# Layer-0 attention scores: the query's low part multiplied through all 128 rows instead of through pairs of 64-row matmuls

## The chip, the cores and the metric

The kernel runs on one core of a Trainium2 chip. The metric is the device time of one execution in microseconds (us), lower is better; of several runs the median is given. The engines are named as in the profile: PE is TensorE (matmuls) and PEld its loading of weights, DVE is VectorE, ACT is ScalarE, POOL is GpSimd, SP is SyncE, which issues most DMAs.

## The reference

A two-layer transformer step over 128 context tokens and 512 latent tokens, width 1024. Layer 0 mixes tokens by differential attention: each of 8 heads has two query/key maps of 64 features, two softmaxes, and the second is subtracted from the first with a factor `lam`.

```python
def block(qb):
    logits = jnp.einsum('bqhmd,bkhmd->bhmqk', qb, k, preferred_element_type=jnp.float32) * scale
    p = jax.nn.softmax(logits, -1)
    a = p[:, :, 0] - lam * p[:, :, 1]
    return jnp.einsum('bhqk,bkhe->bqhe', a, v).astype(v.dtype)
```

Latent queries (4 blocks of 128) see 640 keys: 128 cached context keys and 512 latent ones. Context queries (one block of 128) see the 128 context keys. Layer 1 is a neighbourhood attention with 16 heads of 64 features; each layer ends with an MLP of width 4096.

## The kernel before

All large products are made in three terms: each float32 operand is split into a high part (rounded to the type `fp32r`) and a low part (the rest), and high x high, high x low and low x high are added in one PSUM bank (`mm3`, lines 119 to 121).

For the scores of layer 0 the split is packed into the array's 128 rows, since a map has only 64 features. The tile `K[:, x]` of map `x` holds the key's high part in the 64 rows that belong to the map and its low part in the other 64 rows: "stacked high and low keys". The query tile `q` has four slices. `Q[:, x]` (x is 0 or 1) has the query's high part of map `x` twice, in both halves of the rows; `Q[:, 2 + x]` has the low part of map `x` twice. So one matmul over 128 rows with `Q[:, x]` gives query-high x (key-high + key-low). What is missing, query-low x key-high, comes from a matmul over the 64 rows of the map alone.

`scores0` (line 553) makes one block: 128 queries of one head against 640 keys, for both maps. It takes two PSUM tiles `S` of two banks, one per map, and fills them in two halves of 320 keys, each by a call of `qk`: two matmuls over 128 rows (line 452, map 0 and map 1) and then two over 64 rows (line 454; rows 0 to 63 for map 0, rows 64 to 127 for map 1). There are 8 heads x 4 blocks = 32 such blocks with 8 matmuls each. `ctx_scores0` (line 604) makes the context's block, one call of `qk` with 128 keys, 8 times in all. `softmax0` then reads `S`: a maximum on DVE (line 568), the exponential on ACT (line 570), and small steps on DVE (lines 576 to 578). `trans0` transposes the result on PE (line 589) and splits it on ACT and DVE (lines 126 and 127); `pv0` multiplies it with V.

Layer 0 is not done stage by stage. The order of PE's work is written out by hand in the string `ORDER0`: score blocks (`S`, head, block), transposes (`T`), context scores (`c`), projections of q, k and v (`q`, `v`), rotations of queries and keys (`r`), pieces of the modulation (`m`, `M`) stand mixed. PE's instructions run in that order. The instructions of the other engines are put in order by the framework's scheduler. PE's score blocks run from about 82 to 393 us.

The function `qk` is also called in layer 1 (`scores1`, `ctx_scores1`), where the two low slices are one (`lo` is `(2, 2)`).

Of the kernel before, what the change touches and what calls it, by code (L numbers as in the profile page):

```python
# [18 lines left out]
P = 128  # L19
# [46 lines left out]
class Net:  # L66
# [32 lines left out]
        self.uid += 1  # L99
        return f"{s}_{self.uid}"  # L100

# [1 line left out]

    def run(self, order):
        for name in order.split():
# [6 lines left out]
    def op(self, name, fn, *needs):  # L112
        self.ops[name] = fn, needs

# [1 line left out]

    def mm3(self, out, sh, sl, mh, ml, start, stop):
        te = self.nc.tensor
# [51 lines left out]
        assert m == 48  # L170
        return order

# [1 line left out]

    def pump(self):
        if not self.queue:
# [48 lines left out]
            if kt % 2:  # L225
                self.used(4 * n + kt // 2)

# [1 line left out]

    def consts(self):  # L230
        nc, a, c = self.nc, self.a, self.cst
# [189 lines left out]
            self.done(3)  # L421
        return accs

# [1 line left out]

    def to_h(self, i, src):
        self.split(self.h[0][:, i, :], self.h[1][:, i, :], src)
# [18 lines left out]
            r = HALF[1 - x]  # L446
            nc.gpsimd.tensor_tensor(K[r, x], cr[r, x], K[r, x], ALU.subtract)

    def qk(self, out, Q, K, q, k, lo):
        te = self.nc.tensor  # L450
        for x in range(2):
            te.matmul(out[x], Q[:, x, q], k(K[:, x]), start=True, stop=False)  # L452
        for x, r in enumerate(HALF):
            te.matmul(out[x], Q[r, lo[x], q], k(K[r, x]), start=False, stop=True)  # L454

    def v_evac(self, pool, i, t, src, cache, out):
        def put(slot, s):
# [16 lines left out]
        if t == 4:  # L474
            self.out_copy(pool, src, self.o[out][:, 256 * i : 256 * i + 256], 256)

# [1 line left out]

    def qk0_evac(self, pool, i, t, src):
        nc = self.nc  # L480
# [7 lines left out]
        if t < 4:  # L488
            t2 = pool.tile([P, 256], F32, tag="t2", name=self.nm("t2"))
            five = lambda z: z.rearrange("p (m g s f) -> p m g s f", m=4, g=2, s=2)  # L490
            four = lambda z: z.rearrange("p (a b c) -> p a b c", a=2, b=2)
            s5, d5 = five(src), five(t2)
            n4 = self.sin[:, t].unsqueeze(1).to_broadcast([P, 4, 2, 16])
            c4 = self.cos[:, t].unsqueeze(1).unsqueeze(1).to_broadcast([P, 2, 2, 64])
            nc.vector.tensor_tensor(qk, four(src), c4, ALU.mult)
            nc.vector.scalar_tensor_tensor(d5[:, :, :, 0, :], s5[:, :, :, 1, :], -1.0, n4, ALU.mult, ALU.mult)
            nc.vector.tensor_tensor(d5[:, :, :, 1, :], s5[:, :, :, 0, :], n4, ALU.mult)
            nc.vector.tensor_tensor(qk, qk, four(t2), ALU.add)
            cs = slice(P + P * t, 2 * P + P * t)
        else:  # L500
            nc.scalar.copy(qk, src.rearrange("p (a b c) -> p a b c", a=2, b=2))
            nc.sync.dma_start(self.o["k0"][:, P * i : P * i + P].rearrange("p (a b) -> p a b", b=64), qk[:, 1])
            cs = slice(0, P)
# [49 lines left out]
    def scores0(self, hd, b):  # L553
        K, qs = self.QKs[hd["h"]], slice(P + P * b, 2 * P + P * b)
        s2 = [self.S().rearrange("p (a b) -> p a b", b=512) for _ in range(2)]
        for hf in range(2):
            ks = slice(P + 320 * hf, P + 320 * hf + 320)
            self.qk([s2[m][:, hf, :320] for m in range(2)], self.q0, K, qs, lambda z: z[:, ks], (2, 3))
        hd["E", b] = self.softmax0(hd, b, [s[:, :, :320] for s in s2], 640)

    def softmax0(self, hd, b, s, n):
# [42 lines left out]
    def ctx_scores0(self, hd):  # L604
        K = self.QKs[hd["h"]]
        s = self.S()
        sm = [s[:, 0:P], s[:, 512 : 512 + P]]
        self.qk(sm, self.q0, K, slice(0, P), lambda z: z[:, :P], (2, 3))
        hd["E", 4] = self.softmax0(hd, 4, sm, P)

    def ctx_pv0(self, hd):
# [163 lines left out]
            self.nc.sync.dma_start(X[:, t, :], src[t])  # L775
        return X

# [1 line left out]

    def v1(self, pool, i, t, n, c):  # L780
        m = self.M()
# [60 lines left out]
    def scores1(self, pr, b):  # L842
        nc = self.nc
        Q, K = self.QKs[pr["i"]]
        s = self.S()
        sh = [s[:, 0:384], s[:, 512:896]]
        qs = slice(P * b, P * b + P)
        if b < 3:
            kv, out = lambda z: z[:, P * b : P * b + 384], sh
        else:  # L850
            kv = lambda z: z[:, 0:640].rearrange("p (a b) -> p a b", b=P)[:, 0:5:2, :]
            out = [z.rearrange("p (a b) -> p a b", b=P) for z in sh]
        self.qk(out, Q, K, qs, kv, (2, 2))
        E = pr["E", b]
        mn = self.sml.tile([P, 2], F32, name=self.nm("mn"), tag="mn1")
        Z = self.sml.tile([P, 2], F32, name=self.nm("Z"), tag="Z1")
        for x in range(2):
            nc.vector.tensor_tensor_reduce(
                E[:, x, :], sh[x], E[:, x, :], 1.0, 3.0e38, ALU.add, ALU.min, mn[:, x : x + 1]
            )  # L860
            nc.scalar.activation(E[:, x, :], E[:, x, :], AF.Exp, bias=mn[:, x : x + 1], scale=-1.0, accum_out=Z[:, x : x + 1])
        nc.vector.reciprocal(Z, Z)
        for x in range(2):
            nc.vector.tensor_scalar(E[:, x, :], E[:, x, :], Z[:, x : x + 1], None, ALU.mult)
# [45 lines left out]
    def ctx_scores1(self, pr):  # L910
        nc, pool = self.nc, pr["pool"]
        Q, K = self.QKs[pr["i"]]
        s = self.S()
        sh = [s[:, 0:P], s[:, 512 : 512 + P]]
        qs, ks = slice(NL, NT), slice(640, 768)
        self.qk(sh, Q, K, qs, lambda z: z[:, ks], (2, 2))
        sv = s.rearrange("p (a b) -> p a b", b=512)[:, :, :P]
        mn = self.sml.tile([P, 2], F32, name=self.nm("mn"), tag="mn1")
        Z = self.sml.tile([P, 2], F32, name=self.nm("Z"), tag="Z1")
        E = pr["Ec"] = pool.tile([P, 2, P], F32, tag="Ec", name=self.nm("Ec"), bufs=1)  # L920
        nc.vector.tensor_reduce(mn, sv, AX.X, ALU.min)
        for x in range(2):
            nc.scalar.activation(E[:, x, :], sh[x], AF.Exp, bias=mn[:, x : x + 1], scale=-1.0, accum_out=Z[:, x : x + 1])
        nc.vector.reciprocal(Z, Z)
        nc.vector.tensor_tensor(E, E, Z.unsqueeze(2).to_broadcast([P, 2, P]), ALU.mult)
# [96 lines left out]
            self.pool_lo = 1  # L1022
            return late["X"], first4

# [1 line left out]

    def stats(self, st, X, t, n):
        self.nc.vector.bn_stats(st[:, t, n, :], X[:, t, 512 * n : 512 * n + 512])
# [385 lines left out]
```

## Time and profile before

| | |
|---|---|
| median of 3 runs | 1731.97 us (1730.14 to 1737.19) |
| span of the profiled execution | 1732.1 us |
| PE busy | 1645.9 us (95% of the span) |
| DVE busy | 1131.4 us (65%) |
| ACT busy | 662.1 us (38%) |
| chain that ended last | PE 75%, DVE 14%, issue 4%, POOL 4%, ACT 3% |

The profile is of one execution and gives no time of it other than the span, which lies 0.1 us over the median of the runs; so the span is taken as its time. The start of a matmul in the trace is the moment it begins; its end is modelled, and matmuls overlap in the pipeline, so what a matmul costs is read from the distance between the starts of two that follow each other and not from its duration. A timeline merges instructions of the same line that follow each other into one row with their count. A bracket at a row's end is the engine's idle time before it, with what ended it.

### The profile page before, as it was taken

To read this page: it belongs to the slowest core of one execution; us is meant where nothing else is said; L and a number is where in the kernel's file an instruction comes from. 1 tells how busy PE (TensorE), PEld (TensorE's weight loads), DVE (VectorE), ACT (ScalarE), POOL (GpSimd) and SP (SyncE) were. 2 spreads that over 40 slices of the span, in tenths; PEclk is the share of its full clock that TensorE was granted. 3 is DMA by queue.
4 is the path that set the end of the run, shared out by engine and by line. 5 is a ranking of instruction groups with operands and counts; after the bars stand their busy time and mean duration, and the time that the engine had idled before them with its cause. 6 is when DMAs were issued, how large, how long until landed. Compare 5 with 4: busy or idle time off the path is not lost.

```text
span 1732.1 us, 25928 instructions
## 1 busy us (share of the span) xinstructions
PE 1645.9 (95%) x10026; PEld 1455.4 (84%) x10026; DVE 1131.4 (65%) x2015; ACT 662.1 (38%) x1338; POOL 594.5 (34%) x457
## 2 busy tenths in 40 slices
PE   8999999999699999999998999998889999999997
PEld 5788888777698988989887889997779898898996
DVE  4788778765848789798557577868685343242338
ACT  2456545643531322221324565655353132131321
POOL 2111012113722337154247243342383133424322
PEclk9999999989899999999999999999989999999999
DMA  8432334233144445454223222223123131212221
GB/s 328 147 118 84 100 113 148 80 112 108 57 133 151 159 146 172 142 164 144 77 83 118 89 78 79 77 85 133 61 92 106 59 98 50 97 56 91 81 66 61
DMA packets 59086, 187.96 MB, mean 109 GB/s; under 512 B 7396, under 2 KB 14034, under 8 KB 57938
## 3 DMA queue, kind: packets, MB, share of 16 engines
q1 hardware_dynamic: 55890, 174.89, 31.3%
q0 software_dynamic: 3072, 11.40, 1.8%
q8 instruction: 79, 1.29, 0.3%
q14 instruction: 45, 0.37, 0.1%
HBM read 176.25 MB, written 7.40 MB: 106 GB/s over the span
## 4 chain that ended last, share of the span: by engine, by line
PE 75%; DVE 14%; issue 4%; POOL 4%; ACT 3%; DMA 1%; SPq 0%; DVEq 0%; POOLq 0%; ACTq 0%
PE M L119 14%; PE M L121 14%; PE M L120 14%; PE S L121 8%; PE S L119 7%; PE S L120 7%; DVE wl L196 4%; PE S L452 2%; PE S L454 2%; POOL wl L196 2%; DVE hlo L127 1%; PE M L589 1%; PE M L259 1%; DVE X L1038 1%; POOL X L1078 1%
## 5 line engine op out<-in xcount | busy, mean ns | idle before, releaser
L196 POOL TENSOR_TENSOR wl<-rw,wh 128x512 fp32r<-128x512 f32 x209 | 345.3, 1672 | 591.4 <-ACT wh L194 541.0
L194 ACT CAST wh<-rw 128x1024 fp32r<-128x1024 f32 x192 | 196.9, 1050 | 348.3 <-PE M L121 268.5
L121 PE MATMUL S<-hhi,wl 128*128 128x320 f32 (+1 forms) x944 | 293.4, 311 | 6.1 <-DVE wl L196 4.7
L119 PE MATMUL S<-hhi,wh 128*128 128x320 f32 (+1 forms) x944 | 292.7, 310 | 0.0
L120 PE MATMUL S<-hlo,wh 128*128 128x320 f32 (+1 forms) x944 | 291.9, 309 | 0.0
L119 PE MATMUL M<-wh,uhi 128*128 128x512 f32 x640 | 249.6, 390 | 1.0 <-ACT uhi L126 1.0
L121 PE MATMUL M<-wh,ulo 128*128 128x512 f32 x640 | 249.3, 389 | 0.3
L120 PE MATMUL M<-wl,uhi 128*128 128x512 f32 x640 | 249.2, 389 | 0.0
L196 DVE TENSOR_TENSOR wl<-rw,wh 128x512 fp32r<-128x512 f32 x175 | 208.9, 1213 | 52.3 <-ACT wh L194 51.3
L119 PE MATMUL M<-wh,hhi 128*128 128x256 f32 (+1 forms) x640 | 202.4, 316 | 9.3 <-DVE tmp L1161 8.4
L121 PE MATMUL M<-wh,hlo 128*128 128x256 f32 (+1 forms) x640 | 196.4, 307 | 3.8 <-DVE hlo L127 3.8
L120 PE MATMUL M<-wl,hhi 128*128 128x256 f32 (+1 forms) x640 | 196.2, 307 | 1.8 <-DVE wl L196 1.8
L121 PEld LDWEIGHTS S<-hhi,wl 128*128 128x128 f32 x944 | 178.9, 189 | 10.1 <-DVE wl L196 8.3
L119 PEld LDWEIGHTS S<-hhi,wh 128*128 128x128 f32 x944 | 179.3, 190 | 0.2
L120 PEld LDWEIGHTS S<-hlo,wh 128*128 128x128 f32 x944 | 179.1, 190 | 0.2
L293 DVE SCALAR_TENSOR_TENSOR jk<-wm,cb 128x1024 bf16<-128x1024 f32 x96 | 142.5, 1484 | 1.5
L121 PEld LDWEIGHTS M<-wh,ulo 128*128 128x128 f32 x640 | 120.2, 188 | 26.3 <-DVE ulo L127 1.1
L119 PEld LDWEIGHTS M<-wh,uhi 128*128 128x128 f32 x640 | 120.2, 188 | 26.2 <-ACT uhi L126 1.9
L120 PEld LDWEIGHTS M<-wl,uhi 128*128 128x128 f32 x640 | 120.1, 188 | 24.6
L119 PEld LDWEIGHTS M<-wh,hhi 128*128 128x128 f32 x640 | 124.2, 194 | 18.6 <-DVE tmp L1161 8.9
L1225 DVE SCALAR_TENSOR_TENSOR r<-S,r 128x640 f32<-128x640 f32 (+1 forms) x62 | 48.4, 781 | 137.8 <-ACT r L1224 137.7
L121 PEld LDWEIGHTS M<-wh,hlo 128*128 128x128 f32 x640 | 123.8, 193 | 11.7 <-DVE hlo L127 7.0
(280 smaller groups left out, 3026.6 us busy)
## 6 DMA issues: line engine op xcount, KB each, us to landing
rw<-in_w SPq DMA_DIRECT2D x192, 512.0 KB, 4.2
wm<-in_wmodT SPq DMA_DIRECT2D x48, 512.0 KB, 3.6
rw<-in_wmod SPq DMA_DIRECT2D x32, 512.0 KB, 4.5
wm<-in_wmod SPq DMA_DIRECT2D x8, 1024.0 KB, 10.5
gate<-gates POOLq DMA_DIRECT2D x6, 512.0 KB, 5.0
X<-in_xT SPq DMA_DIRECT2D x8, 320.0 KB, 11.1
X<-in_xn SPq DMA_DIRECT2D x5, 512.0 KB, 5.4
x<-X SPq DMA_DIRECT2D x5, 512.0 KB, 2.8
```

The costliest lines, as they stand in the source:

```text
L119: te.matmul(out, sh, mh, start=start, stop=False)
L120: te.matmul(out, sh, ml, start=False, stop=False)
L121: te.matmul(out, sl, mh, start=False, stop=stop)
L127: nc.vector.tensor_tensor(lo, src, hi, ALU.subtract)
L194: keep(nc.scalar.copy(hi, r))
L196: keep(eng.tensor_tensor(lo[:, k], r[:, k], hi[:, k], ALU.subtract))
L259: self.nc.tensor.matmul(acc[32 * j : 32 * j + 32, :256], self.sc[:, 4 * r + j, :], w[:, j, :], start=r == 0, stop=r == 1, tile_position=(0 ...
L293: op = nc.vector.scalar_tensor_tensor(jk, ws[t], 1.0, cb[:, x, :], ALU.mult, ALU.mult, accum_out=mc[:, t, x : x + 1])
L452: te.matmul(out[x], Q[:, x, q], k(K[:, x]), start=True, stop=False)
L454: te.matmul(out[x], Q[r, lo[x], q], k(K[r, x]), start=False, stop=True)
L589: nc.tensor.transpose(t[:, P * (j - j0) : P * (j - j0) + P], E[:, P * j : P * j + P], self.idf)
L1225: nc.vector.scalar_tensor_tensor(rv, src, 0.0, rv, ALU.max, ALU.mult)
```

## The change

`qk` now makes, for each map in turn, two matmuls over all 128 rows: one with the query's high slice and one with its low slice, both against the stacked keys. The 64-row form lives on as `qk_rows`, for layer 1 alone, with the same instructions as before. In place of query-low x key-high the new form adds query-low x (key-high + key-low). The tiles, what is written into them, and the order string stay.

```diff
-    def qk(self, out, Q, K, q, k, lo):
+    def qk(self, out, Q, K, q, k):
+        te = self.nc.tensor
+        for x in range(2):
+            te.matmul(out[x], Q[:, x, q], k(K[:, x]), start=True, stop=False)
+            te.matmul(out[x], Q[:, 2 + x, q], k(K[:, x]), start=False, stop=True)
+
+    def qk_rows(self, out, Q, K, q, k):
         te = self.nc.tensor
         for x in range(2):
             te.matmul(out[x], Q[:, x, q], k(K[:, x]), start=True, stop=False)
         for x, r in enumerate(HALF):
-            te.matmul(out[x], Q[r, lo[x], q], k(K[r, x]), start=False, stop=True)
+            te.matmul(out[x], Q[r, 2, q], k(K[r, x]), start=False, stop=True)
...
-            self.qk([s2[m][:, hf, :320] for m in range(2)], self.q0, K, qs, lambda z: z[:, ks], (2, 3))
+            self.qk([s2[m][:, hf, :320] for m in range(2)], self.q0, K, qs, lambda z: z[:, ks])
...
-        self.qk(sm, self.q0, K, slice(0, P), lambda z: z[:, :P], (2, 3))
+        self.qk(sm, self.q0, K, slice(0, P), lambda z: z[:, :P])
...
-        self.qk(out, Q, K, qs, kv, (2, 2))
+        self.qk_rows(out, Q, K, qs, kv)
```

On PE the first score block (head 0, block 0) stands so before; `S_915` is the PSUM tile of map 0, `S_916` that of map 1, and `M_909` and `M_943` belong to the transposes around the block:

```order
L268 MATMUL M_909<-idf,X_549 128x128 x2
L452 MATMUL S_915<-K_751,q_546 128x320
L452 MATMUL S_916<-K_751,q_546 128x320
L454 MATMUL S_915<-K_751,q_546 128x320
L454 MATMUL S_916<-K_751,q_546 128x320
L452 MATMUL S_915<-K_751,q_546 128x320
L452 MATMUL S_916<-K_751,q_546 128x320
L454 MATMUL S_915<-K_751,q_546 128x320
L454 MATMUL S_916<-K_751,q_546 128x320
L513 MATMUL M_943<-idf,X_549 128x128 x3
```

and so after it, where line 453 is the low part through 128 rows:

```order
L268 MATMUL M_909<-idf,X_549 128x128 x2
L452 MATMUL S_915<-K_751,q_546 128x320
L453 MATMUL S_915<-K_751,q_546 128x320
L452 MATMUL S_916<-K_751,q_546 128x320
L453 MATMUL S_916<-K_751,q_546 128x320
L452 MATMUL S_915<-K_751,q_546 128x320
L453 MATMUL S_915<-K_751,q_546 128x320
L452 MATMUL S_916<-K_751,q_546 128x320
L453 MATMUL S_916<-K_751,q_546 128x320
L519 MATMUL M_943<-idf,X_549 128x128 x3
```

The count stays at eight; the last two now belong to map 1, so that map 0 is whole two matmuls before the block's end. The scheduler's order on DVE differs in two places. At the first, near 293 us, it stood so before; `AB_105` and `mc_99` are the modulation's columns, `mx_3621` the maxima of a score block, `q_546` and `K_3633` the next queries and keys:

```order
L334 TENSOR_TENSOR AB_105<-one_4316,lnc 128x16
L335 TENSOR_TENSOR AB_105<-AB_105,mc_99 128x16
L568 TENSOR_REDUCE mx_3621<-S_3611 128x1
L568 TENSOR_REDUCE mx_3621<-S_3612 128x1
L517 SCALAR_TENSOR_TENSOR q_546<-M_3639,q_546 128x2x128
L519 TENSOR_TENSOR K_3633<-M_3639,K_3633 64x128 x2
L270 TENSOR_REDUCE red_3651<-M_3648 128x4
L576 RECIPROCAL Z_3622<-Z_3622 128x1
L275 TENSOR_TENSOR mc_99<-red_3651,bm_119 128x4
```

and so after, with line numbers six higher from there on:

```order
L334 TENSOR_TENSOR AB_105<-one_4316,lnc 128x16
L574 TENSOR_REDUCE mx_3621<-S_3611 128x1
L574 TENSOR_REDUCE mx_3621<-S_3612 128x1
L270 TENSOR_REDUCE red_3651<-M_3648 128x4
L335 TENSOR_TENSOR AB_105<-AB_105,mc_99 128x16
L275 TENSOR_TENSOR mc_99<-red_3651,bm_119 128x4
L523 SCALAR_TENSOR_TENSOR q_546<-M_3639,q_546 128x2x128
L525 TENSOR_TENSOR K_3633<-M_3639,K_3633 64x128 x2
L582 RECIPROCAL Z_3622<-Z_3622 128x1
```

Three small instructions of the modulation changed places with the maxima and the next rotation. The second place, near 331 us, is of the same kind (three steps of a rotation and the steps of the normalisation between them). On ACT two casts of a key change places with their neighbours; on POOL and SP the order is the same.

## Rows read from the trace of the kernel before

**Rows 1.** The page: the span, PE's line of busy time, and DVE's busy tenths in 40 slices of 43.3 us each.

```profile
span 1732.1 us, 25928 instructions
PE 1645.9 (95%) x10026; PEld 1455.4 (84%) x10026; DVE 1131.4 (65%) x2015; ACT 662.1 (38%) x1338; POOL 594.5 (34%) x457
...
DVE  4788778765848789798557577868685343242338
```

**Rows 2.** Busy time of each engine in the stretch from 80 to 394 us; the column after the engines is the granted clock, then the DMA engines' share and GB/s.

```profile
80.00:394.00 314.00, 303.04 (x2184) 253.37 (x2184) 244.42 (x613) 171.79 (x438) 50.51 (x46) 0.97 0.34 110
```

**Rows 3.** Groups of instructions by line and shape, from 80 to 394 us: line, engine, operation, tiles, shapes, count; busy us, mean ns of one; idle time before them and what ended it.

```profile
L452 PE MATMUL S<-K,q 128*128 128x320 f32 x128 | 34.9, 352 | 0.9 <-ACT E L570 0.9
L454 PE MATMUL S<-K,q 64*128 64x320 f32 x128 | 26.5, 410 | 0.0
...
L568 DVE TENSOR_REDUCE mx<-S 128x1 f32<-128x640 f32 x64 | 50.6, 817 | 10.0 <-PE S L454 9.4
```

**Rows 4.** PE's timeline over a score block that comes after projection matmuls: start us, us, instruction, count.

```profile
87.72 0.45 PE L452 MATMUL S<-K,q 128*128 128x320 f32 x2
88.10 0.41 PE L454 MATMUL S<-K,q 64*128 64x320 f32 x2
88.45 0.56 PE L452 MATMUL S<-K,q 128*128 128x320 f32 x2
88.94 0.41 PE L454 MATMUL S<-K,q 64*128 64x320 f32 x2
89.28 0.55 PE L513 MATMUL M<-idf,nt 128*128 128x128 f32 x3
```

**Rows 5.** PE's timeline over a score block that comes after transposes, and the transposes behind it.

```profile
128.76 0.53 PE L452 MATMUL S<-K,q 128*128 128x320 f32 x2
129.23 0.41 PE L454 MATMUL S<-K,q 64*128 64x320 f32 x2
...
130.41 0.44 PE L268 MATMUL M<-idf,rows 128*128 128x128 f32 x2
130.68 0.49 PE L513 MATMUL M<-idf,X 128*128 128x128 f32 x3
131.01 0.38 PE L268 MATMUL M<-idf,X 128*128 128x128 f32 x2
```

**Rows 6.** PE's timeline in the MLP, matmuls over 128 rows with 320 columns, each with weights of its own; the first and the last of 13 in a row, 12 steps apart.

```profile
619.77 0.31 PE L121 MATMUL S<-hhi,wl 128*128 128x320 f32 x1
...
621.53 0.31 PE L121 MATMUL S<-hhi,wl 128*128 128x320 f32 x1
```

**Rows 7.** PE's timeline over a context block of scores (128 keys): its first row and the row behind it.

```profile
202.30 0.33 PE L452 MATMUL S<-K,q 128*128 128x128 f32 x2
...
202.82 0.55 PE L513 MATMUL M<-idf,X 128*128 128x128 f32 x3
```

**Rows 8.** All waits of PE from 80 to 394 us: who waited for whom, us in total, times, longest.

```profile
PE M L513 <- DVE aT L127: 3.8, 1, 3.8
PE M L624 <- DVE red L270: 2.0, 1, 2.0
PE M L120 <- DVE wl L196: 1.8, 2, 1.3
PE M L121 <- DVE hlo L127: 1.7, 1, 1.7
PE S L452 <- ACT E L570: 0.9, 1, 0.9
PE M L589 <- DVE K L519: 0.2, 1, 0.2
PE M L589 <- DVE E L578: 0.2, 1, 0.2
```

**Rows 9.** DVE's timeline: the rows at which DVE last came out of an idle time of 0.15 us or more before six of the waits on it.

```profile
143.81 0.29 DVE L127 TENSOR_TENSOR aTc<-M,aTc 128x128 fp32r<-128x128 f32 x1 [0.28 <-ACT aTc L126]
...
168.89 0.16 DVE L625 COPY ssq<-M 128x5 f32<-128x5 f32 x1 [0.40 <-PE M L624]
...
210.40 0.89 DVE L127 TENSOR_TENSOR aT<-M,aT 128x512 fp32r<-128x512 f32 x2 [2.65 <-ACT aT L126]
...
260.40 0.69 DVE L127 TENSOR_TENSOR aT<-M,aT 128x512 fp32r<-128x512 f32 x1 [0.56 <-ACT aT L126]
...
270.68 0.42 DVE L127 TENSOR_TENSOR V<-M,V 128x256 fp32r<-128x256 f32 x1 [0.31 <-ACT V L126]
...
336.98 0.42 DVE L495 TENSOR_TENSOR nt<-M,cos 128x256 f32<-128x256 f32 x1 [0.79 <-PE M L121]
```

**Rows 10.** PE's timeline: the first row of the score block that lies between each of these rows and the wait that follows it.

```profile
147.04 0.39 PE L452 MATMUL S<-K,q 128*128 128x320 f32 x1
...
168.71 0.54 PE L452 MATMUL S<-K,q 128*128 128x320 f32 x2
...
209.55 0.54 PE L452 MATMUL S<-K,q 128*128 128x320 f32 x2
...
264.78 0.45 PE L452 MATMUL S<-K,q 128*128 128x320 f32 x2
...
273.50 0.45 PE L452 MATMUL S<-K,q 128*128 128x320 f32 x2
...
339.98 0.45 PE L452 MATMUL S<-K,q 128*128 128x320 f32 x2
```

More of the change, by code (lines that the diff above doesn't have):

```diff
@@ L915, in ctx_scores1 @@
         qs, ks = slice(NL, NT), slice(640, 768)
-        self.qk(sh, Q, K, qs, lambda z: z[:, ks], (2, 2))
+        self.qk_rows(sh, Q, K, qs, lambda z: z[:, ks])
         sv = s.rearrange("p (a b) -> p a b", b=512)[:, :, :P]
```

## The prediction

> **What bounds the kernel now.** I read the page first, then the busy time of the stretch that holds the score blocks, then the waits in it, and only then single blocks. On the page PE is busy for 95% of the span [rows 1]; that alone says little, since a matmul's end is modelled. The stretch from 80 to 394 us says more: PE is busy for 303.0 of 314 us, DVE for 244.4 (78%), ACT for 171.8 [rows 2]. PE waited there on other engines eight times, 10.6 us in all, nearly always on DVE [rows 8]. So PE's own stream sets the time of about 97% of the stretch, and DVE is second, close enough to count. The other way round, DVE waited on finished scores for 9.4 us [rows 3]. No row has PE waiting for a DMA. Behind 394 us nothing is changed, and what PE gains before should arrive at the end whole.
>
> **The change, part by part.** It takes 64 pairs of 64-row matmuls with 320 columns (128 single ones [rows 3]) and 8 pairs with 128 columns, one for each head's context block, out of PE's stream, and puts one matmul over 128 rows in for each of the 144 single ones. No DMA, no tile and no evacuation is added.
>
> *One block before.* From the first matmul to the next work: 87.72 to 89.28, 1.56 us [rows 4]; after transposes 128.76 to 130.41, 1.65 us [rows 5]. The second is longer only at its start: its first two matmuls take 0.47 us where those of the first block take 0.38, and that difference belongs to the transposes ahead and stays. Inside a block the two matmuls of a pair start together (both begin in one row of 0.41 us, the mean of one is 410 ns [rows 3, 4]), but the switch costs on both sides: 0.35 us from a pair to the next full matmul, 0.49 us for the two full matmuls behind a pair [rows 4]. The work behind the block pays too: two transposes right behind a pair take 0.27 us (130.41 to 130.68), where three later ones take 0.33 (130.68 to 131.01), 0.11 each; so 0.05 us more [rows 5].
>
> *One block after.* Eight matmuls over 128 rows with 320 columns, each with new weights. The MLP has such a stream: 12 steps from 619.77 to 621.53, 0.147 us each [rows 6]. The load of each matmul's weights is in that step. Eight steps are 1.18 us. The gain is 1.56 - 1.18 = 0.38 us, and 0.05 behind it: 0.43. Over 32 blocks 13.8 us.
>
> *Context blocks.* Before 0.52 us [rows 7]. After, four matmuls of 128 columns at the 0.11 us that transposes of that shape keep [rows 5]: 0.44. With the 0.05 behind them 0.13 us, eight times: 1.0 us. Together 14.8 us of PE time.
>
> *What DVE takes back.* Where PE waits on a DVE that has not been idle since before the block, the shorter block only lengthens that wait. DVE's last idle times before six of the waits end at the rows of [rows 9], and in each of those stretches stands one score block [rows 10]: 6 x 0.43 = 2.6 us lost. Ahead of the wait on the exponential I take off one context block, 0.1 us. The other 26 blocks lie before a point where DVE itself waits for PE, or for ACT that waits for PE, so DVE moves up with them. How many waits appear that the trace lacks it cannot show. They lie between none and one for every second remaining block, 13 x 0.43 = 5.6 us; DVE would then be at 244.4 of some 307 us, 80%, against 78% now. I take 1 us, nearer to none, since PE's existing waits are eight in 40 blocks.
>
> *Edits at nothing.* Map 0 is whole two matmuls before the end of its block; its maximum (0.82 us a piece [rows 3]) can start up to 0.29 us sooner relative to that end. Counted at nothing, between 0 and a gain of 0.29 us at each of the eight waits, 2.3 us. The swapped modulation steps on DVE are a few tenths of a microsecond each in a stretch with idle time ahead of them; if that cover failed, less than 1 us. PSUM banks are filled by two matmuls in a row in place of alternating; the MLP's stream does that already at 0.147 us.
>
> *Sum.* 14.8 - 2.7 - 1.0 = 11.1 us. The span is 1732.1 us [rows 1] and the runs' median 1731.97, so both give 1721 us.
>
> **A rule against it, and one for it.** The pair's two matmuls share one slot [rows 3, 4]. The Trainium skill (TensorE: Matmul & The Clock Gate, Part 3: Packing small matmuls) says the same: matmuls in different row groups run at the same time. By that rule alone a block would go from six slots to eight and lose about 0.29 us as an estimate, which with 32 blocks ends near 1741; the trace agrees with the overlap and not with the conclusion, and I count it with rival 3. The missing piece is in the rows too: the steps around a pair are 0.35 and 0.49 us. The skill (TensorEngine Tiling (Array Packing), Key Properties) has it that a change of tiling mode drains the array; the trace agrees, and by it the sum stands as above.
>
> **The rivals.**
> 1. *DVE becomes the bound* in more places. For it: DVE stands at 7 and 8 tenths through the stretch [rows 1] and all but one of PE's waits name it. Against: DVE waited 9.4 us on scores [rows 3]. With every second remaining block lost: 14.8 - 2.7 - 5.6 = 6.5, so 1725.5 us.
> 2. *DVE takes back nothing*, because map 0's earlier maximum shortens just those chains. For it: 0.29 us sooner against 0.43 us less. Against: in the stretches of [rows 9] DVE has no idle time to use. 14.8 us gained and some of the waits shorter: 1717 us.
> 3. *Slower.* The 0.49 us for two full matmuls [rows 4] may not be the switch but how score matmuls run with these keys and queries, 0.245 us each. Then eight take 1.96 us against 1.56 + 0.05: 0.35 us lost, 32 times, 11 us: 1743 us. It decides from 0.20 us per matmul on ((1.56 + 0.05) / 8). Against: the first two matmuls of the block at 87.72 take 0.38 us up to the pair, less than 0.49 although the drain before the pair is in it.
> That the change does not do what it says can be left out: PE's order shows the new stream.
>
> **How the numbers follow.** Forecast 0.60, rival 1 0.24, rival 2 0.12, rival 3 0.04. The predicted time is 1721. The range goes from 1716 (rival 2 with one of its gains) to 1727.5 (rival 1 with two more microseconds lost to waits); rival 3 is left out. A difference under 0.5%, 8.7 us, is what a measurement of this kernel can hardly tell from none; the line lies at 1723.3. The forecast's own spread, 1718 to 1724, is almost all below it. So faster 0.55 + 0.12 + a small part of rival 1, 0.70; same 0.26; slower 0.04.
>
> **What would show it.** Right: score matmuls of lines 452 and 453 start 0.147 us apart inside a block, a block takes about 1.18 us to the next work (1.27 behind transposes), weight loads in it show no idle time, the stretch from the first block to the last is shorter by about 11 us, and the rest of the trace is the same length. PE's waits on DVE grow from 10.6 to some 14 us. Wrong in the sum: steps of 0.2 us or more. Wrong in what DVE takes back: waits on DVE that grow by over 6 us, or don't grow at all. Wrong altogether: a gain or a loss that lies behind 394 us.

## The result, and the profile after

The changed kernel takes 1721.06 us (median of 4 runs, 1719.74 to 1723.43); the kernel before, in runs made beside it, 1731.13 us (4 runs, 1730.14 to 1737.19). The ratio is 0.9928 with a 95% interval of 0.991 to 0.9946, a gain of 0.5% to 0.9%. The prediction was 1721.0.

The profiled execution of the changed kernel lasted 1720.29 us with a span of 1718.5, so 1.8 us lie around the span; the other three runs show the same difference. The profile of before (span 1732.1) therefore belongs to an execution of about 1733.9 us, above its median. That is why the two profiles lie 13.6 us apart and the medians only 10.1.

From the page of the changed kernel, the lines that answer to [rows 1], and the shares of the chain that ended last:

```profile
span 1718.5 us, 25925 instructions
...
PE 1630.8 (95%) x10026; PEld 1461.4 (85%) x10026; DVE 1130.0 (66%) x2015; ACT 662.0 (39%) x1338; POOL 594.6 (35%) x457
...
PE 72%; DVE 15%; issue 4%; POOL 4%; ACT 3%; DMA 2%; SPq 0%; DVEq 0%; POOLq 0%; ACTq 0%
```

PE is 15.1 us less busy, DVE 1.4. PE still bounds the kernel; its share of the chain fell from 75% to 72%, DVE's rose from 14% to 15%.

A block of scores after projection matmuls, and the row behind it, in PE's timeline (start us, us, instruction, count), against [rows 4]:

```profile
88.19 0.30 PE L452 MATMUL S<-K,q 128*128 128x320 f32 x1
88.33 0.31 PE L453 MATMUL S<-K,q 128*128 128x320 f32 x1
88.48 0.31 PE L452 MATMUL S<-K,q 128*128 128x320 f32 x1
...
89.36 0.49 PE L519 MATMUL M<-idf,nt 128*128 128x128 f32 x3
```

Eight even steps: 88.19 to 89.36 is 1.17 us, 0.147 each, where the block took 1.56 before. A block that follows transposes, and the transposes behind it, against [rows 5]:

```profile
127.24 0.39 PE L452 MATMUL S<-K,q 128*128 128x320 f32 x1
127.47 0.31 PE L453 MATMUL S<-K,q 128*128 128x320 f32 x1
...
128.50 0.38 PE L268 MATMUL M<-idf,rows 128*128 128x128 f32 x2
128.71 0.49 PE L519 MATMUL M<-idf,X 128*128 128x128 f32 x3
```

It takes 1.26 us (before 1.65); the first step is the long one (0.23), as it was. The two transposes behind take 0.21 us in place of 0.27, so the excess behind a pair is gone too. The context block, against [rows 7]:

```profile
197.98 0.22 PE L452 MATMUL S<-K,q 128*128 128x128 f32 x1
...
198.37 0.51 PE L519 MATMUL M<-idf,X 128*128 128x128 f32 x3
```

0.39 us, before 0.52. The length of the whole stretch is read from two rows in each timeline: the first matmul of the first score block and the matmul behind the last. Before:

```profile
82.64 0.54 PE L452 MATMUL S<-K,q 128*128 128x320 f32 x2
...
393.00 0.33 PE L119 MATMUL M<-aTc,V 128*128 128x128 f32 x1
```

After:

```profile
83.45 0.39 PE L452 MATMUL S<-K,q 128*128 128x320 f32 x1
...
381.37 0.33 PE L119 MATMUL M<-aTc,V 128*128 128x128 f32 x1
```

310.36 us before, 297.92 after: 12.4 us shorter. The rest of the 13.6 lies outside. The first block starts 0.8 us later in the trace of after. At the start of layer 1, between 950 and 970 us of the trace of before, that execution lost about 1.9 us that the other didn't (part of it is a wait of 0.9 us on a weight's cast). Neither place is touched by the change.

All waits of PE in that stretch of the changed kernel, from 80 to 384 us (who waited for whom, us in total, times, longest), against [rows 8]:

```profile
PE M L519 <- DVE aT L127: 3.8, 1, 3.8
PE M L120 <- DVE wl L196: 2.5, 2, 1.8
PE M L630 <- DVE red L270: 2.0, 1, 2.0
PE M L121 <- DVE hlo L127: 1.7, 1, 1.7
PE M L595 <- DVE K L525: 0.9, 2, 0.6
PE S L452 <- ACT E L576: 0.8, 1, 0.8
PE M L595 <- DVE E L584: 0.7, 2, 0.3
PE M L519 <- ACT o L620: 0.5, 1, 0.5
PE M L259 <- PE M L519: 0.2, 1, 0.2
PE S L119 <- ACT E L576: 0.2, 1, 0.2
```

Summed unrounded they are 13.2 us. The same sum was 10.7 before, 2.5 us less: 10.5 for the waits of [rows 8], and 0.2 for one that answers to the last row here and lies just behind 394 us. The work behind them is unchanged. DVE is busy for 244.5 us, as before (244.4 [rows 2]), now in 304 us (80 to 384).

A bracket of idle time says less than the wait costs. It begins at the modelled end of the matmul ahead, some 0.3 us after that matmul's start, where a stream without waits has its next start after 0.147 us. The block ahead of the wait on `E` in [rows 10], before:

```profile
264.78 0.45 PE L452 MATMUL S<-K,q 128*128 128x320 f32 x2
...
266.60 0.66 PE L589 MATMUL M<-idf,E 128*128 128x128 f32 x4 [0.16 <-DVE E L578]
```

and after:

```profile
258.18 0.30 PE L452 MATMUL S<-K,q 128*128 128x320 f32 x1
...
260.15 0.66 PE L595 MATMUL M<-idf,E 128*128 128x128 f32 x4 [0.35 <-DVE E L584]
```

The bracket grew by 0.19 us, but the block, which should be 0.39 us shorter, is 0.15 us longer (1.97 in place of 1.82): 0.54 us went back here.

DVE's own wait for scores shrank, from 9.4 us before the maxima [rows 3] to 3.0 in the groups of after (busy us, mean ns | idle before and what ended it):

```profile
L574 DVE TENSOR_REDUCE mx<-S 128x1 f32<-128x640 f32 x64 | 50.4, 815 | 3.2 <-PE S L453 3.0
L452 PE MATMUL S<-K,q 128*128 128x320 f32 x128 | 40.3, 325 | 0.8 <-ACT E L576 0.8
L453 PE MATMUL S<-K,q 128*128 128x320 f32 x128 | 38.1, 308 | 0.0
```

The busy time of the score matmuls is larger than before (78.4 us against 61.4), while they finish sooner: their modelled durations overlap, and only the distance between starts tells what they cost.

### The profile page after: what moved, and what is told of

Its sections match the earlier page's. It is cut to its first block, busy times and chain, and to the rows that moved or that the text cites. A ratio compares the mean times of both kernels' runs of the same rounds, so it can differ in the third digit from the quotient of the medians.

```text
span 1718.5 us, 25925 instructions
## 1 busy us (share of the span) xinstructions
PE 1630.8 (95%) x10026; PEld 1461.4 (85%) x10026; DVE 1130.0 (66%) x2015; ACT 662.0 (39%) x1338; POOL 594.6 (35%) x457
## 4 chain that ended last, share of the span: by engine, by line
PE 72%; DVE 15%; issue 4%; POOL 4%; ACT 3%; DMA 2%; SPq 0%; DVEq 0%; POOLq 0%; ACTq 0%
PE M L119 14%; PE M L121 14%; PE M L120 14%; PE S L121 8%; PE S L119 7%; PE S L120 7%; DVE wl L196 4%; POOL wl L196 2%; DVE hlo L127 1%; DVE X L1044 1%; POOL X L1084 1%; PE M L259 1%; PE M L595 1%; PE M L884 1%; POOL X L1085 1%
## 5 line engine op out<-in xcount | busy, mean ns | idle before, releaser
L121 PEld LDWEIGHTS S<-hhi,wl 128*128 128x128 f32 x944 | 179.1, 190 | 10.1 <-DVE wl L196 8.3
```

What stands on the lines that cost most here:

```text
L121: te.matmul(out, sl, mh, start=False, stop=stop)
```

## The experiments

The diffs below are against the changed kernel, unless the text says otherwise; `...` stands for lines left out. Theory: switching between 128-row and 64-row matmuls cost PE 0.43 us a block, and DVE, second in the stretch, takes back part of what that frees. The runs with the old order and with one switch separate this from the new order of the two maps and from the 64-row form itself.

**Once more.** The changed kernel unaltered, beside the next three.

> The changed kernel once more, beside the three below on the same chip. Theory (switch): each change between 128-row and 64-row matmuls costs PE time (the array runs empty, and the next load of weights is not hidden), and that is what the change takes out; DVE gives some 2.5 us of it back as longer waits. Then 1721 us, 10 to 11 us under the kernel before. Rival (order): the gain comes from the new order, two matmuls in a row into one PSUM bank and map 0 whole sooner; it gives the same time here and parts from the theory in the next run.

Measured: 1722.88 us against 1734.74 for before, ratio 0.9932 [0.992, 0.9945]. The result repeats. The score stretch is 298.5 us here.

**The old order of the maps.** All matmuls over 128 rows, but both maps' high parts first, as before.

```diff
         for x in range(2):
             te.matmul(out[x], Q[:, x, q], k(K[:, x]), start=True, stop=False)
+        for x in range(2):
             te.matmul(out[x], Q[:, 2 + x, q], k(K[:, x]), start=False, stop=True)
```

> All matmuls over 128 rows as in the changed kernel, but in the order of the kernel before: both maps with the query's high part, then both with its low part. Switch: steps of 0.147 us as in the changed kernel, the same time within 1 us, 1721. Order: the gain goes, or a part of it: 2 us if map 0's earlier maximum matters at PE's waits (1723), all of it if the order is the cause (1731).

Measured: 1721.43 us, 0.9923 [0.9911, 0.9935]; the stretch is 299.5 us. The same as the change within the intervals: that map 0 is whole sooner, and that one bank is filled by two matmuls in a row, is worth nothing that can be measured.

**One switch a block, 64-row pairs kept.** The four matmuls over 128 rows first, then both 64-row pairs; context blocks as before.

```diff
...
+        te, kss = self.nc.tensor, [slice(P + 320 * hf, P + 320 * hf + 320) for hf in range(2)]
+        for hf, ks in enumerate(kss):
+            for x in range(2):
+                te.matmul(s2[x][:, hf, :320], self.q0[:, x, qs], K[:, x, ks], start=True, stop=False)
+        for hf, ks in enumerate(kss):
+            for x, r in enumerate(HALF):
+                te.matmul(s2[x][:, hf, :320], self.q0[r, 2 + x, qs], K[r, x, ks], start=False, stop=True)
...
```

> The 64-row pairs of the kernel before, but in each block of 640 keys first the four matmuls over 128 rows and then the two pairs: one switch forth and back per block in place of two. Context blocks as in the kernel before. Switch: a block takes 3 x 0.147 + 0.238 + 0.147 + 0.340 = 1.17 us to the next work, as short as eight full matmuls, with 0.05 us behind it; so 32 x 0.38 = 12 us of PE time saved, less 2.5 on DVE: 1722 us. Rival (the 64-row form is slow in itself, not the switch): all 64 pairs are still there, nothing or little is saved: 1730.

Measured: 1723.07 us, 0.993 [0.9918, 0.9941]; the stretch is 299.5 us. All 64 pairs are still there, and nearly the whole gain has come. PE's timeline over the block after the first projections:

```profile
86.30 0.74 PE L566 MATMUL S<-K,q 128*128 128x320 f32 x4
86.97 0.57 PE L569 MATMUL S<-K,q 64*128 64x320 f32 x4
87.47 0.55 PE L520 MATMUL M<-idf,nt 128*128 128x128 f32 x3
```

The block takes 1.17 us. Four full matmuls up to the first pair are 0.67 us (0.59 at 0.147, so 0.08 for the switch), two pairs 0.50, 0.25 each: less than two full matmuls at 0.147. The step from the first pair (86.97) to the second (87.22) is as long as the other, though the form does not change there. So a switch is paid in two steps: about 0.09 us ahead of the first matmul of the new form and 0.10 behind it. (The expectation had 0.147 and 0.340 for the last two steps; only their sum was right.) Of the 0.39 us that a block had lost inside itself, all comes back when the two pairs stand together; the 0.06 us behind a block and the context blocks' part don't, and the medians don't show that difference. So the 64-row form was not what cost time; going to it and back twice a block was.

**A switch at every matmul.** The 64-row matmuls are kept, but each follows its own full one, so that no two of them form a pair.

```diff
-        for x in range(2):
+        for x, r in enumerate(HALF):
             te.matmul(out[x], Q[:, x, q], k(K[:, x]), start=True, stop=False)
-            te.matmul(out[x], Q[:, 2 + x, q], k(K[:, x]), start=False, stop=True)
+            te.matmul(out[x], Q[r, 2 + x, q], k(K[r, x]), start=False, stop=True)
```

> The kernel before with its 64-row matmuls taken apart: in layer 0 each follows its own matmul over 128 rows, so that the array changes form at every matmul. The count of matmuls is the same. Switch: from full to row 0.34 us, from row to full 0.34 us, so a half block is 4 x 0.34 = 1.37 us and a block 2.7 in place of 1.6; 32 blocks 36 us, context blocks about 4 more, less up to 5 us of waits that go: some 1766 us. Rival (the 64-row form is slow in itself): at most the lost overlap, 0.15 us per pair: 72 x 0.15 = 11 us, 1742.

Measured: 1763.44 us against 1733.47 for before, 1.0173 [1.0152, 1.0193], 30 us slower. In PE's timeline the end of a block:

```profile
90.96 0.41 PE L452 MATMUL S<-K,q 128*128 128x320 f32 x1
91.31 0.41 PE L453 MATMUL S<-K,q 64*128 64x320 f32 x1
91.65 0.55 PE L519 MATMUL M<-idf,nt 128*128 128x128 f32 x3
```

Every step but the block's first (0.23) is 0.34 us, in both directions, against 0.147 in a stream without switches. Each holds the second part of one switch and the first part of the next: 0.19 us for a switch at this shape. The Trainium skill (TensorEngine Tiling (Array Packing), Key Properties) has it that changing the tiling mode drains the engine; the trace agrees, at 0.19 us a switch. What happens at a switch is seen in the weight loads (PEld). In the kernel before, the loads for the pair at 88.10 [rows 4] are

```profile
88.10 0.19 PEld L454 LDWEIGHTS S<-K,q 64*128 64x128 f32 x2 [0.19 <-issue]
```

and in the changed kernel the load for the matmul at 88.48 is

```profile
88.34 0.19 PEld L452 LDWEIGHTS S<-K,q 128*128 128x128 f32 x1
```

At the switch the load begins only when its own matmul does, after PEld has stood idle; without a switch it begins 0.14 us earlier, beside the matmul ahead. In the whole stretch PEld idles for 12.7 us ahead of the loads of line 454 before, and for 0.2 us ahead of those of line 453 after. In this run the block takes 2.63 us (from 89.02), 1.07 more than before. PE's waits from 80 to 420 us in this kernel:

```profile
PE M L519 <- DVE aT L127: 3.0, 1, 3.0
PE M L121 <- DVE hlo L127: 1.7, 1, 1.7
PE M L630 <- DVE red L270: 0.8, 1, 0.8
...
PE M L120 <- DVE wl L196: 0.2, 1, 0.2
```

This is the take-back seen from its other side: with longer blocks the waits fall to 6.0 us, 4.7 under before. The one on `red` goes from 2.0 to 0.8, the longer one on `wl` from 1.3 to 0.2, the one on `aT` from 3.8 to 3.0, each by about what the one block ahead of it grew (1.07). The wait on `hlo`, with no block between it and the wait on `aT` before, stays at 1.7.

**Low parts moved from DVE to POOL.** In layer 0's attention both steps of a pair that make a weight's low part (`wl`) run on POOL, once on the changed kernel and once, by the same edit, on the kernel before.

```diff
-            self.pool_lo = 1
+            self.pool_lo = 2
```

> The changed kernel, but in layer 0's attention the low halves of the weights are made on POOL alone, in place of one half on DVE and one on POOL: this takes some 20 instructions of 1.25 us off DVE between 80 and 394 us. If DVE takes back PE's gain there as the prediction has it, PE's waits on DVE (13.2 us in the changed kernel) shrink by several us and the time with them: 1715 to 1719. Rival (POOL's slower half becomes the wait): waits on POOL appear in place of those on DVE: 1721 or later.

> The same edit on the kernel before. It measures the change's worth with DVE relieved: by the prediction's terms the change is worth 14.8 us of PE time, of which 2.5 come back as waits; with fewer waits the distance between this run and the one above should be 13 to 15 us, against 10 to 12 between the two kernels as they are. If the distance stays at 11, the waits on DVE are not what takes the rest.

Measured: 1731.72 us (0.9991 [0.9982, 1.0]) on the changed kernel and 1741.86 (1.0047 [1.0033, 1.0062]) on the one before, against 1733.47 for before. The edit makes the kernel before 8.4 us slower. The changed kernel is 9 to 11 us slower than in its runs above, which were made on other chips, where 1715 to 1719 was expected; the distance between the two was expected at 13 to 15 us and is 10.1. The first lines of PE's waits from 80 to 396 us, on the changed kernel, say why:

```profile
PE M L119 <- DVE aT L127: 9.1, 1, 9.1
PE M L120 <- POOL wl L196: 6.7, 12, 0.7
```

POOL makes these parts in 1.38 us each when they stand in a row (five in 6.89 us at 269.78), later than PE wants them, and PE waits about 0.6 us twelve times. The wait on `aT`, 9.1 us now, bears DVE's name but comes from POOL too. One row of DVE's timeline and two of POOL's:

```profile
347.97 0.89 DVE L726 SCALAR_TENSOR_TENSOR X<-X,sub 128x640 f32<-128x640 f32 x1 [3.76 <-DMA X<-rnd]
...
334.93 8.60 POOL L196 TENSOR_TENSOR wl<-rw,wh 128x512 fp32r<-128x512 f32 x6 [1.93 <-issue]
343.47 0.55 POOL L725 DMA_DIRECT2D X<-rnd  x1
```

DVE stands idle for 3.76 us, with `aT` right behind in its order, until a transfer has landed; POOL issues that transfer, and only after six low parts in a row. In the changed kernel POOL issues it at 339.53 and DVE doesn't wait for it; on the kernel before with this edit DVE idles 5.7 us there and the wait on `aT` is 11.0. So the rival held. DVE is relieved of 17 us and PE waits 19.8 in place of 13.2. These two runs don't test the take-back, since waits on POOL, or on what POOL issues, took the place of those on DVE in both; that a busy engine's work can go to an idle one without loss was wrong here. That the distance is still 10.1, though the waits of the two differ by only 0.9 us (18.9 and 19.8), is explained in part, for the two profiled executions: 23.9 us of the score stretch ran at a granted clock of 0.5 with the change and 13.7 without, and PE's steps there, the wait on `aT` aside, account for 4.4 us. Whether the other runs share that is not shown.

**Less DVE work by a smaller maximum.** To relieve DVE without loading another engine.

```diff
-            nc.vector.tensor_reduce(mx[:, m : m + 1], s[m], AX.XY if n > P else AX.X, ALU.max, negate=True)
+            nc.vector.tensor_reduce(mx[:, m : m + 1], s[m][..., :8], AX.XY if n > P else AX.X, ALU.max, negate=True)
+            nc.vector.tensor_scalar(mx[:, m : m + 1], mx[:, m : m + 1], 1.0 / 64, None, ALU.mult)
...
-                bias=mx[:, m : m + 1],
+                bias=mx[:, m : m + 1], scale=1.0 / 64,
```

> Leaves out most of the row maximum of layer 0's softmax: DVE reduces 8 keys of each half in place of 320, and a small second step scales the result by 1/64, as the exponential does too, so the weights are those of another temperature. That takes about 64 x 0.65 = 42 us of DVE's work out of the changed kernel's score stretch (busy 244 of 304 us there, so about 200). Theory (DVE took back 2.5 us of the gain of about 14.9): PE's waits on DVE before the score blocks' end fall from 13.2 to a few us, and this kernel ends 14 to 15 us under the same edit of the kernel before. Rival (DVE takes nothing back; the gain that reaches the end is about 11 to 12 for another reason, such as the clock or transfers): the distance stays at 10 to 12 us, though DVE's waits go.

> The same edit on the kernel before (the same part is left out). Both theories: PE's waits from 80 to 394 us fall from 10.7 to a few us, and the time falls by 3 to 9 us against the kernel before. Theory: the distance to the changed kernel with the same edit is 14 to 15 us; rival: 10 to 12 us.

Measured: 1731.63 us (0.9989 [0.998, 0.9998]) and 1746.54 (1.0067 [1.005, 1.0084]) against 1734.05. The distance, 14.9 us, is the theory's number, but not for the theory's reason: both kernels became slower, and PE's waits did not go. The first of them on the changed kernel with this edit, from 80 to 396 us:

```profile
PE M L519 <- DVE gr L316: 4.5, 1, 4.5
PE S L452 <- DVE K L525: 3.4, 2, 2.3
PE M L119 <- DVE aT L127: 3.2, 1, 3.2
```

DVE is busy for 217.8 us of that window, 27 less than in the stretch without the edit, and PE waits for 21.9 us in place of 13.2, partly at other steps (`gr`, `K` ahead of scores). DVE's order is another one: `aT` stands behind `gr` here (349.81 and 344.34), with 1.4 us of DVE idle for a transfer between them, and ahead of it without the edit (337.76 and 339.22); there PE waits 3.8 us for `aT`, here 4.5 for `gr` and 3.2 for `aT`. That the scheduler chose this order because the maximum is shorter is likely, but not shown. Between the two kernels with the edit the score stretch shrinks by 12.1 us (319.3 to 307.2) with 2.6 us more waits (19.3 to 21.9, each with one wait just behind the stretch), just as it did without the edit; the rest of the 14.9 is not explained by the stretch. What the pair shows is that less load on DVE does not by itself shorten these waits. That they follow from where a step stands in DVE's order fits, but was followed up at this one place only.

**Layer 1 as well.** Layer 1's scores through 128 rows too. Its query tile gets a fourth slice; one DVE step of double width writes both low slices, and the copies between the halves carry them along. To make room the exponential's buffers go from 6 to 5 and one small tile shares another's place.

```diff
-            Q = pool.tile([P, 3, NT], F32R, tag="Q", name=self.nm("Q"), bufs=2)
+            Q = pool.tile([P, 4, NT], F32R, tag="Q", name=self.nm("Q"), bufs=2)
...
-                nc.vector.scalar_tensor_tensor(Q[:, 2, c], src, -0.125, Q[:, 0, c], ALU.mult, ALU.subtract)
+                nc.vector.scalar_tensor_tensor(
+                    Q[:, 2:4, c], src.unsqueeze(1).to_broadcast([P, 2, k]), -0.125, Q[:, 0:2, c], ALU.mult, ALU.subtract
+                )
...
-                    nc.sync.dma_start(Q[HALF[1 - y], y, :].bitcast(F32), Q[r, y, :].bitcast(F32))
+                    nc.sync.dma_start(Q[HALF[1 - y], y : y + 3 : 2, :].bitcast(F32), Q[r, y : y + 3 : 2, :].bitcast(F32))
...
-        E = pool.tile([P, 2, 384], F32, tag="E", name=self.nm("E"), bufs=6)
+        E = pool.tile([P, 2, 384], F32, tag="E", name=self.nm("E"), bufs=5)
...
-        self.qk_rows(out, Q, K, qs, kv)
+        self.qk(out, Q, K, qs, kv)
...
```

> The changed kernel, with layer 1's scores through 128 rows as well: its query tile gets a fourth slice, the low part is written twice by one DVE instruction of double width and copied to the other rows by the DMAs that copy the high part; one buffer fewer for the bias tiles makes room. Switch: a block of 384 keys takes 4 x 0.174 = 0.70 us in place of 0.82, with 0.07 us less behind it, 32 times, and the context blocks 0.15 us less, 8 times: 7 us of PE time, so 1714 us if DVE and the DMAs hide what is added, and a few us more if they don't. Rival (DVE): DVE's wider splits, some 32 x 0.25 us, come back as waits: 1721 or later.

Measured: 1717.96 us, 0.9907 [0.9892, 0.9921]; beside it, on the same chip, the changed kernel has 1722.88. It is the fastest version, 4.9 us under the change by these medians. A block of layer 1 in PE's timeline of the changed kernel:

```profile
1013.96 0.52 PE L458 MATMUL S<-K,Q 128*128 128x384 f32 x2
...
1014.78 0.41 PE L119 MATMUL M<-hhi,wh 128*128 128x320 f32 x1
```

and of this one:

```profile
1013.46 0.34 PE L452 MATMUL S<-K,Q 128*128 128x384 f32 x1
...
1014.16 0.31 PE L119 MATMUL M<-hhi,wh 128*128 128x320 f32 x1
```

0.82 us for the block and 0.10 too much in the step behind it (the next matmul starts at 1015.03, 0.25 later) became 0.70 and none (0.14): 0.22 us, 7.0 over 32 blocks if all are like this one. PE's first two waits in layer 1, from 940 to 1240 us, are

```profile
PE M L886 <- DVE E L872: 4.7, 3, 3.4
PE S L452 <- DVE mn L866: 3.2, 4, 1.6
```

where the changed kernel has 2.9 and 1.2 us at these places. So 3.8 of the 7 us go back to DVE here, a larger share than in layer 0, and the time lies between the expectation (1714) and its rival (1721); DVE also has 5.3 us more to do (its low-part steps take 15.3 us in place of 10.0).

**Both edits together.** Layer 1 as above, and the low parts on POOL.

> Layer 1's scores through 128 rows as well, and layer 0's low halves of weights on POOL: the two gains are in different stretches and should add: 3 to 4 us under the run with layer 0's low halves on POOL alone.

Measured: 1727.94 us, 0.997 [0.9959, 0.9981], 3.8 us under the POOL edit alone, as expected, and near the 4.9 without that edit: no sign that the gain in layer 1 depends on what happens in layer 0.

## Why the prediction was right

- *PE's own time.* The prediction had 0.43 us a block, in steps of 0.147. Measured: 0.38 to 0.39 inside a block and about 0.06 behind it. The context block was taken at 0.08 inside and 0.05 behind; it gave 0.12 and 0.04, since its steps are 0.10 us and not the 0.11 of transposes. Outside the score blocks PE runs the same order in both traces, so that steps and blocks can be matched one to one. By those that no wait touches, the gain over all 32 and 8 blocks and the steps behind them is 15.2 us, where 14.8 was predicted.
- *The stretch.* It is 12.4 us shorter where 11.1 was forecast, and the rest is luck of the execution: 17.1 us of it ran at a granted clock of 0.5 (1.2 GHz) after and 20.5 before, and the matched steps give 1.3 us for that. 15.2 less 3.8 given back (the next point), 1.3 more for the clock and 0.3 less in small differences make the 12.4. In the two traces that have the half clock of before (20.5 us: the old order, layer 1 too) the stretch is 10.8 and 11.1 us shorter; in the repeat and with one switch (13.7 us each) it is 11.9 and 10.9, the first with a wait of 1.2 us on a transfer, the second with less PE time saved.
- *What DVE takes back.* Predicted 2.7 us at known waits and 1.0 at new ones, 3.7 in all. By the idle times it is 2.5. Start to start, in the matched steps and blocks at which PE idles in either trace, it is 3.8, in the trace of layer 1 too as in that of after. The split was not quite as told. By the idle times, of the six waits the two on `wl` grew by 0.3 and 0.5, those on `K` and `E` by 0.2 each, and the one on `aT` not at all, but a wait of 0.5 on `o` appeared just ahead of it; the one on `red` stayed at 2.0, because the two low-part steps ahead of it on DVE ran in 3.14 us in place of 3.46. That makes 1.6 in place of 2.7. New waits (`E`, `K`, a tile of PE's own) add 1.1, and the waits on the exponential lost 0.2. The mechanism, a block shortened behind a DVE that isn't idle, is shown from the other side by the waits that shrank when the blocks were lengthened.
- *Nothing for map 0's order and for the banks.* Right: the old order gives the same time.
- *Steps moved on DVE.* Right: DVE's busy time is unchanged. The rotation at the second moved place has one of the new waits behind it (`K`, 0.57 us), but from the step on `E` ahead of it to its end it takes 3.30 us (320.90 to 324.20) where it took 3.22 (329.60 to 332.82), so the new order has 0.08 of that wait at most.
- *Rival 1* (5.6 us to new waits, 8.3 in all) and *rival 2* (nothing taken back) are both excluded, by 2.5 as by 3.8. *Rival 3* needed steps of 0.20 us; they are 0.147.
- *From the trace to the median.* This step had a small fault: the span of before was taken as its time, but 1.8 us lie around a span. By that the profiled execution of before took about 1733.9 us, and the same 11.1 us would have ended near 1723 from it. From the median, 1731.97, they end at 1721, and that is the line that should have been given alone. The profiles differ by 13.6 us because two places that the change doesn't touch fell in its favour by 1.1 us net, and the stretch by 12.4. That the median fell within 0.1 us of the prediction is luck: single runs of the changed kernel spread over 3.7 us, and the difference to before was 10.1 us here, 11.9 in the repeat and 13.3 with the old order.

What stays open: what the remaining 2.8 us between the two kernels with the smaller maximum are, and how much the half clock has in the distance of the two with the low parts on POOL.

## What to carry over

Look at the distance between the starts of matmuls around a change of the row count, not at the small matmul itself: here the packed pair was cheap and the switches around it cost more than two full matmuls. If the operands can be laid out for the full array, drop the packing; if not, put all packed matmuls of a block together so that it switches once. And when PE becomes faster, find the waits behind which the feeding engine isn't idle and count the blocks ahead of them: that, not its busy share, says what is given back.

## What was not expected

- A switch between 128-row and 64-row matmuls of 320 columns costs 0.19 us in either direction (0.34 us a step against 0.147), and it falls in two steps: 0.09 us ahead of the first matmul of the new form, 0.10 behind it.
- Taking work off DVE made PE wait longer, with DVE's work moved (19.8 us, POOL's 1.38 us steps in a row) and with it left out (21.9 us, DVE busy for 27 us less), against 13.2. In the first case POOL, newly loaded, also issued a transfer late, and DVE stood idle for it with a step behind that PE wanted.
- Waits repeat to hundredths of a microsecond between executions and even between kernels: the one on `aT` is 3.83 us in the trace of before, of after, of the repeat and of the old order.
